# Sixteen-row triangular inverses in quads of rows, in a two-layer decoder trunk

## The chip, the cores and the metric

The kernel runs on one core of a Trainium2 chip. The metric is the device time of one execution in microseconds (us). Before the change it is 1115.59 us, the median of three runs (1115.23 to 1119.18 us).

Five engines work side by side on the core: PE (TensorE, matrix products, with its weight loads listed as PEld), DVE (VectorE), ACT (ScalarE), POOL (GpSimd) and SP (SyncE, which here only issues DMA transfers). Each engine executes its own instructions strictly in the order in which the program lists them, so an instruction that waits holds up everything listed behind it on the same engine.

## The reference

The program computes a decoder trunk of two layers over a sequence of 1024 tokens with 1024 channels. The even layer runs two mixers side by side: an RWKV-7 time mixing (8 heads of 64 channels) and a chunked spatial gate; the odd layer is a sliding-window attention. The change touches the RWKV-7 part alone, whose core is a recurrence over time:

```python
def step(S, inp):
    r_t, w_t, k_t, v_t, kk_t, a_t = inp
    sa = jnp.einsum('bhvk,bhk->bhv', S, -kk_t)
    S = (S * w_t[:, :, None, :]
         + sa[..., None] * (kk_t * a_t)[:, :, None, :]
         + v_t[..., None] * k_t[:, :, None, :])
    y_t = jnp.einsum('bhvk,bhk->bhv', S, r_t)
    return S, y_t
```

The kernel does not step through time. It cuts the sequence into chunks of 64 tokens, and inside a chunk the term with `sa` makes every token depend on the ones before it through a unit lower triangular 64 x 64 matrix. That matrix has to be inverted once per chunk and head. The inverse is built from 16 x 16 diagonal blocks, which are inverted first, and put together by matrix products. How the 16 x 16 blocks are inverted is what changes.

## The kernel before

**The stages.** The first 100 us load x, the conditioning and the first weights. From about 100 us to 630 us the even layer's input projections and the RWKV-7 and gate mixers run together. From 630 us on come the even layer's output projection (tile `op`), the odd layer's projections and attention, and the last output projection.

**The units.** The RWKV-7 work is cut into eight units: four pairs of heads times two halves of the sequence (512 tokens, eight chunks). Each unit goes through `front` (elementwise preparation of tiles `BK`, `AR`, `SV`, `BR`, `PA`), `solve` (the triangular inverse), `prep`, `scan` (the hop from chunk to chunk through PSUM tile `chain`) and `post`.

**The solve of a unit.** PE makes the 64 x 64 matrices (tiles `A` and `pM`). ACT copies the diagonal 16 x 16 blocks into `Dg`. DVE transposes them into `LN` (L638), picks `Lf` out of it (L643, L644), sets its diagonal to one (L645), and then goes through the rows 1 to 15: one `tensor_tensor` product of the row of `Lf` with the inverse's rows so far, written to the scratch tile `pr` (L650), and one `tensor_reduce` that sums it into row i of the inverse `LT` (L651). Each instruction needs the one before it. Then DVE transposes to `Tm`, masks to `ZT` (L655) and transposes to `Zq` (L658). PE multiplies (`pM<-ZT,Dg`), ACT copies to `M0`, PE multiplies again (`pM<-Zq,M`), DVE adds into `Zq` (L680) and transposes to `Tq` (L682), and PE goes on with `pM<-Tq,N`. The unit's matrices lie on the 128 partitions, 16 x 16 elements per partition for `Lf` and 16 x 8 for `LT`.

**What sets the order.** PE's instructions are listed in an order that the program plans itself while it is built. `drive()` runs nine generator threads by priority; a thread that has issued some work yields the delay after which it wants to go on, read from the table `LAT`, on a planner's clock that counts only the matrix products issued. While the solve thread is waiting, the lowest thread, `stream()`, fills in projection products (`pproj`, three per weight block, 128 x 512). The entry `qt2` is the delay between the product that the solve issues first (`p<-SV,AV`, L118) and `pM<-ZT,Dg`, that is, the time that the planner allows for the DVE's inverse. The order on DVE, ACT, POOL and SP is made by the framework's scheduler, which gives the instructions of front, solve, prep and post a higher priority than the rest.

**The other names that the prediction uses.** The gate mixer's thread makes `gvn` (normalisation, finished on DVE by `vn`, L826), `lnb` and `mix` (finished on DVE by `mx`, L841, and `uT`, L842) on PE. A thread for the conditioning loads rows of `ada` into one buffer (`araw`, L854), adds them up on DVE (`adacc`, L857) and sends the sum through PE (`adac`, `adag`; the latter is copied out by ACT as `adacc`, L868). All of `gvn`, `lnb`, `mix`, `adac` and `adag` write to one single PSUM buffer (tag "g"), so each has to wait until the one before has been read. In `front`, `kt`, `kb` and `bkt` are PE transposes of tiles that DVE makes. The output projection `op` starts as soon as the projections are through; its inputs `whi`/`wlo` are split by ACT (L245) and DVE (L246) from `wraw`, which is loaded from `y0d` in DRAM.

Of the kernel before, what the change touches and what calls it, by code (L numbers as in the profile page):

```python
# [11 lines left out]
F32 = mybir.dt.float32  # L12
# [3 lines left out]
ALU = mybir.AluOpType  # L16
AX = mybir.AxisListType
# [3 lines left out]
P = 128  # L21
# [33 lines left out]
NC2 = CONSTS["alibi"]  # L55


LAT = {"debt": 0.7, "share": 0.4, "p1": 2.31, "uw": 3.0, "mq": 4.0, "f0": 0.5, "sv0": 4.0, "wo": 2.31, "x1": 6.0, "yf": 7.85, "fetch": 3.85, "unit_norm": 12.0, "c81": 4.0, "qt1": 1.5, "bkt": 1.0, "qt2": 20.0, "qt3": 1.65, "qt4": 1.77, "qt5": 1.2, "qt6": 1.0, "yn": 12.0, "gm_tail1": 1.0, "gm_tail2": 12.0, "lnb": 1.0, "do_ada1": 4.5, "pick1": 0.5, "hop": 1.3, "ada": 8.0}


def _consts():
    c = np.zeros((P, NCON), np.float32)

    def put(name, a):
        c[:, CONSTS[name]:CONSTS[name] + a.shape[1]] = a

    r = np.arange(P)
    blk = (r[:, None] // 64) == (r[None, :] // 64)
    put("ident", np.eye(P))
    put("cblk", np.eye(P) - blk / 64.0)  # L70
    put("oblk", blk)
    s = r[:, None] % 64
    t = np.arange(64)[None, :]
    put("mr", t >= s)
    put("ma", t > s)
    rep = r % 32 // 16
    lt = np.zeros((P, 16, 8))
    for ch in range(8):
        lt[r, rep + 2 * ch, ch] = 1.0
    put("lt16", lt.reshape(P, 128))  # L80
    lane = r % 16 // 8
    put("m01", np.stack([lane == 0, lane == 1], 1))
    put("bm", np.stack([rep == 0, rep == 1], 1))
    put("tri", r[None, :] >= r[:, None])
    put("sel", np.stack([r < 64, r >= 64], 1))
    q = np.arange(128)[:, None]
    kj = np.arange(256)[None, :]
    dist = q + 128 - kj
    put("alibi", np.where((dist >= 0) & (dist < 128), dist, BIG))
    return c  # L90


@with_exitstack
def tile_kernel(ctx, tc, x, cons, par, rows, ada, ada0, ew, wup, sgw, sgb, ewo, ow, owo, out, dbg=None):
# [29 lines left out]
    V = nc.vector  # L124
# [341 lines left out]
    rsol = res.enter_context(tc.tile_pool(name="rsol", bufs=1, side="right", reuse_waits="tile"))  # L466
# [133 lines left out]
    def solve(un):  # L600
# [14 lines left out]
        for g in range(2):  # L615
            cg = slice(g * 4, g * 4 + 4)
            pts = [pm("A"), pM()]
            for i in range(4):
                c = g * 4 + i
# [3 lines left out]
            for hd in range(2):  # L623
                os = rows2[1 - hd]
                p4 = pts[hd].rearrange("p (c t) -> p c t", t=P)
# [11 lines left out]
        LN = rsol.tile([P, 16, 32], F32, name="LN", tag="LN", bufs=1)  # L637
        V.transpose(LN, Dg.rearrange("p x t -> p t x").unsqueeze(2).to_broadcast([P, 16, 2, 16]))  # L638
        LT = rsol.tile([P, 16, 8], F32, name="LT", tag="LT", bufs=1)
        S.activation(LT.rearrange("p a b -> p (a b)"), RC("lt16", 128), AF.Copy)  # L640
        m01 = RC("m01", 2)
        Lf = qt("Lf")
        V.tensor_scalar(out=Lf, in0=LN[:, :, 0:16], scalar1=m01[:, 0:1], scalar2=None, op0=ALU.mult)  # L643
        V.scalar_tensor_tensor(out=Lf, in0=LN[:, :, 16:32], scalar=m01[:, 1:2], in1=Lf, op0=ALU.mult, op1=ALU.add)  # L644
        V.memset(Lf.rearrange("p a b -> p (a b)")[:, 0:256:17], 1.0)  # L645
        LTt = LT.rearrange("p i c -> p c i")
        for i in range(1, 16):
            nc_ = i // 2 + 1
            pr = rsol.tile([P, 8, 16], F32, name="pr", tag="pr", bufs=1)
            V.tensor_tensor(out=pr[:, 0:nc_, 0:i + 1], in0=Lf[:, i:i + 1, 0:i + 1].to_broadcast([P, nc_, i + 1]), in1=LTt[:, 0:nc_, 0:i + 1], op=ALU.mult)  # L650
            V.tensor_reduce(out=LT[:, i, 0:nc_], in_=pr[:, 0:nc_, 0:i + 1], axis=AX.X, op=ALU.add)  # L651
        Tm = qt("Tm")
        V.transpose(Tm.rearrange("p x (k r) -> p k r x", r=2), LTt.unsqueeze(2).to_broadcast([P, 8, 2, 16]))
        ZT = qt("ZT", (8, 32))
# [1 line left out]
                        in1=RC("bm", 2).unsqueeze(2).unsqueeze(3).to_broadcast([P, 2, 8, 16]), op=ALU.mult)  # L656
# [10 lines left out]
        p1 = pM()  # L667
        p2 = p1[:, 256:384].rearrange("p (c t) -> p c t", t=16)
        for c in range(8):
            for qd in range(4):  # L670
                a = qd * 32
# [4 lines left out]
        for c in range(8):  # L676
            for qd in range(4):
                a = qd * 32
# [15 lines left out]
        p1 = pM()  # L694
        p1v = p1.rearrange("p (c t) -> p c t", t=64)
        for c in range(8):
            for hd in range(2):
                a, b = hd * 64, hd * 64 + 32
# [5 lines left out]
        for c in range(8):  # L704
            for hd in range(2):
                a, b = hd * 64, hd * 64 + 32
# [587 lines left out]
    wo = []  # L1294
# [116 lines left out]
```

## Time and profile before

| | |
|---|---|
| runs (us) | 1115.59, 1119.18, 1115.23 |
| the profiled execution (us) | 1115.7 |
| its span, first to last instruction (us) | 1113.9 |
| mean granted TensorE clock | 0.979 |
| PE busy | 1031.2 us, 93% of the span |
| DVE busy | 720.1 us, 65% |
| ACT busy | 526.3 us, 47% |
| POOL busy | 389.0 us, 35% |

In an answer of the profile a row of instructions reads: start in us from the beginning of the span, duration in us, engine, line of the source, operation, output tile <- input tiles, shape, how many were merged (x...), and in brackets how long the engine stood idle before it and what ended that. A row of waits reads: engine, instruction and line <- what it waited for: us in total, how often, the longest. Consecutive matrix products overlap, so a row's duration can be longer than the distance to the next row. The profiled time (1115.7 us) is its span plus 1.8 us, and lies 0.1 us above the median of the runs.

### The profile page before, as it was taken

What the parts mean: (1) busy time and instruction counts of PE and PEld (TensorE: products, weight loads), DVE (VectorE), ACT (ScalarE), POOL (GpSimd) and SP (SyncE); (2) the same over time, 40 slices, a digit from 0 to 9 for tenths busy, and PEclk for the clock granted to TensorE, in tenths of its full rate; (3) what the DMA queues carried; (4) which work ended last, traced back from release to release, by engine and by line L of the source; (5) the groups of instructions that cost most, each with busy time, mean ns of one, the idle gap of its engine ahead of it and who ended that gap; (6) DMA issues with size and microseconds to landing.
All of it is one profiled execution on the core that took longest, in us unless ns stands there. A gap on an engine that the chain in (4) does not pass through costs nothing.

```text
span 1113.9 us, 20597 instructions
## 1 busy us (share of the span) xinstructions
PE 1031.2 (93%) x7800; PEld 839.5 (75%) x7800; DVE 720.1 (65%) x1682; ACT 526.3 (47%) x1252; POOL 389.0 (35%) x490
## 2 busy tenths in 40 slices
PE   3899898899998998989999899999999999989997
PEld 2677676777776786767878688878888888878886
DVE  5865858595869585694744576764565644478754
ACT  5575434554454435544332322335565644487521
POOL 3642414240335122252423200034554544467201
PEclk8799999999999999999999899999999999999999
DMA  8710212112222121123324443321110111252121
GB/s 304 271 27 20 77 59 67 44 63 67 68 79 65 58 86 49 58 69 121 96 73 155 143 142 123 123 72 39 39 39 20 39 39 38 72 165 70 65 94 56
DMA packets 55130, 93.41 MB, mean 84 GB/s; under 512 B 5748, under 2 KB 15988, under 8 KB 55032
## 3 DMA queue, kind: packets, MB, share of 16 engines
q1 hardware_dynamic: 45032, 77.10, 21.3%
q10 hardware_dynamic: 10000, 15.01, 4.1%
q8 instruction: 61, 1.00, 0.4%
q14 instruction: 37, 0.30, 0.1%
HBM read 79.49 MB, written 12.59 MB: 83 GB/s over the span
## 4 chain that ended last, share of the span: by engine, by line
PE 71%; DVE 17%; ACT 5%; issue 3%; DMA 3%; POOL 2%; ACTq 0%; POOLq 0%; SPq 0%; DVEq 0%
PE pproj L118 35%; PE op L118 16%; DVE acc L371 2%; PE po L118 2%; PE pS L118 2%; PE pT L1222 2%; PE pM L118 2%; DVE pr L650 2%; PE py L118 1%; ACT Dg L632 1%; PE uw L118 1%; PE pn L118 1%; DVE LT L651 1%; PE chain L118 1%; PE A L118 1%
## 5 line engine op out<-in xcount | busy, mean ns | idle before, releaser
L118 PE MATMUL pproj<-hi,whi 128*128 128x512 f32 x704 | 284.5, 404 | 0.7 <-ACT vt L1176 0.7
L118 PE MATMUL pproj<-lo,whi 128*128 128x512 f32 x704 | 284.0, 403 | 0.0
L118 PE MATMUL pproj<-hi,wlo 128*128 128x512 f32 x704 | 283.4, 403 | 0.0
L246 POOL TENSOR_TENSOR wlo<-wraw,whi 128x512 fp32r<-128x512 f32 x86 | 114.7, 1353 | 181.2 <-ACT whi L245 180.3
L118 PEld LDWEIGHTS pproj<-hi,whi 128*128 128x128 f32 x704 | 133.7, 190 | 26.8 <-issue 1.7
L118 PEld LDWEIGHTS pproj<-hi,wlo 128*128 128x128 f32 x704 | 133.3, 189 | 25.2 <-issue 1.0
L118 PEld LDWEIGHTS pproj<-lo,whi 128*128 128x128 f32 x704 | 133.5, 190 | 24.4 <-issue 0.9
L245 ACT ACTIVATE whi<-wraw 128x512 fp32r<-128x512 f32 x102 | 58.7, 622 | 66.8 <-PE htp L122 31.6
L118 PE MATMUL op<-wo,whi 128*128 128x512 f32 x256 | 81.9, 401 | 0.0
L1212 ACT ACTIVATE Sx<-Sx,nm 128x257 f32<-128x257 f32 (+1 forms) x128 | 62.3, 489 | 27.2 <-DVE nm L1208 25.1
L1208 DVE CUSTOM_DVE_ANT_0 Sx<-pS,bias,nsink 128x256 f32<-128x256 f32 (+1 forms) x128 | 53.5, 463 | 30.4 <-PE pS L118 29.2
L1216 POOL TENSOR_SCALAR Sx<-Sx,rc 128x256 f32<-128x256 f32 (+1 forms) x128 | 60.8, 491 | 26.3 <-DVE rc L1214 23.7
L1228 DVE TENSOR_TENSOR PL<-pT,PH 128x512 fp32r<-128x512 f32 (+1 forms) x64 | 41.6, 655 | 30.1 <-ACT PH L1227 29.5
L118 PEld LDWEIGHTS op<-wo,whi 128*128 128x128 f32 x256 | 48.8, 191 | 11.8 <-issue 0.3
L857 DVE SCALAR_TENSOR_TENSOR adacc<-araw,cond,adacc 128x512 f32<-128x512 f32 x56 | 47.1, 840 | 11.3 <-DMA araw<-ada 11.1
L118 PE MATMUL op<-hi,yl 128*128 128x512 f32 (+1 forms) x136 | 51.7, 380 | 0.4 <-DVE yl L1327 0.4
L118 PE MATMUL op<-hi,yh 128*128 128x512 f32 (+1 forms) x136 | 51.7, 380 | 0.4 <-ACT yh L1326 0.4
L118 PE MATMUL op<-wo,wlo 128*128 128x512 f32 x128 | 51.9, 405 | 0.2 <-DVE wlo L246 0.2
L118 PE MATMUL op<-lo,yh 128*128 128x512 f32 (+1 forms) x136 | 51.6, 379 | 0.0
L213 POOL TENSOR_TENSOR st<-st,nhalf 128x1 f32<-128x1 f32 x16 | 10.4, 652 | 104.9 <-DVE st L212 104.9
L650 DVE TENSOR_TENSOR pr<-Lf,LT 128x2 f32<-128x2 f32 (+14 forms) x120 | 43.8, 365 | 2.6
L1227 ACT ACTIVATE PH<-pT 128x512 fp32r<-128x512 f32 (+1 forms) x64 | 35.7, 563 | 17.7 <-PE pT L1222 16.4
(311 smaller groups left out, 2172.1 us busy)
## 6 DMA issues: line engine op xcount, KB each, us to landing
araw<-ada SPq DMA_DIRECT2D x64, 256.0 KB, 2.7
wraw<-ew SPq DMA_DIRECT2D x50, 256.0 KB, 3.1
wraw<-ow SPq DMA_DIRECT2D x36, 256.0 KB, 2.8
adaraw<-ada SPq DMA_DIRECT2D x16, 512.0 KB, 4.8
x<-x SPq DMA_DIRECT2D x8, 512.0 KB, 6.7
woraw<-ewo SPq DMA_DIRECT2D x16, 256.0 KB, 3.0
xr<-x ACTq DMA_DIRECT2D x16, 256.0 KB, 3.1
wraw<-y0d SPq DMA_DIRECT2D x16, 256.0 KB, 3.1
```

The source lines that it names most:

```text
L118: last[0] = nc.tensor.matmul(out, lhsT=lhsT, rhs=rhs, **kw).ins
L245: a = S.activation(hi[:, gs, :], raws[g], AF.Copy)
L246: b = E.tensor_tensor(out=lo[:, gs, :], in0=raws[g], in1=hi[:, gs, :].bitcast(F32), op=ALU.subtract)
L371: V.scalar_tensor_tensor(out=acc, in0=raw[:, i], scalar=c, in1=acc, op0=ALU.mult, op1=ALU.add)
L650: V.tensor_tensor(out=pr[:, 0:nc_, 0:i + 1], in0=Lf[:, i:i + 1, 0:i + 1].to_broadcast([P, nc_, i + 1]), in1=LTt[:, 0:nc_, 0:i + 1], op=ALU ...
L857: op = V.scalar_tensor_tensor(out=acc, in0=raw, scalar=cond[:, k:k + 1], in1=acc, op0=ALU.mult, op1=ALU.add)
L1208: V.tensor_tensor_reduce(out=Sx[:, e, off:2 * P], in0=pS3[:, e, 0:nk], in1=bias[e][:, off:], scale=1.0, scalar=nsink[:, hd:hd + 1], op0=AL ...
L1212: S.activation(pr[:, e, off:2 * P + 1], Sx[:, e, off:2 * P + 1], AF.Exp, bias=nm[:, e:e + 1], scale=-1.0, accum_out=sm[:, e:e + 1])
L1216: G.tensor_scalar(out=pr[:, e, off:2 * P], in0=pr[:, e, off:2 * P], scalar1=rc[:, e:e + 1], scalar2=0.5, op0=ALU.mult, op1=ALU.mult)
L1222: nc.tensor.transpose(pT4[:, kb, e, :], pr[:, e, kb * P:(kb + 1) * P], ident)
L1227: S.activation(PH[:, ks, :], pT2[:, ks, :], AF.Copy)
L1228: V.tensor_tensor(out=PL[:, ks, :], in0=pT2[:, ks, :], in1=PH[:, ks, :].bitcast(F32), op=ALU.subtract)
```

## The change

Fifteen rows, one after the other, become four quads of rows. First the diagonal of `Lf` is set to zero, and with three more memsets what lies above it inside each 4 x 4 diagonal block. Then rows are combined so that each quad's own 4 x 4 block is resolved in `Lf` itself: one product and one add for odd rows from even rows, and for each of two columns two products and one add for the last two rows of each quad from its first two (eight instructions, over all quads at once). The diagonal is set to one. Then each quad needs one product over its four rows and all columns up to its end (4 x n x w elements, with w = 4, 8, 12, 16 and n = 2, 4, 6, 8, so 32, 128, 288 and 512) and one `tensor_reduce`. The scratch is now the tile `LN`, whose contents are used up by then. The planner's entry `qt2` goes from 20.0 to 18.

```diff
--- before.py
+++ after.py
@@ -55,7 +55,7 @@
 NC2 = CONSTS["alibi"]
 
 
-LAT = {"debt": 0.7, "share": 0.4, "p1": 2.31, "uw": 3.0, "mq": 4.0, "f0": 0.5, "sv0": 4.0, "wo": 2.31, "x1": 6.0, "yf": 7.85, "fetch": 3.85, "unit_norm": 12.0, "c81": 4.0, "qt1": 1.5, "bkt": 1.0, "qt2": 20.0, "qt3": 1.65, "qt4": 1.77, "qt5": 1.2, "qt6": 1.0, "yn": 12.0, "gm_tail1": 1.0, "gm_tail2": 12.0, "lnb": 1.0, "do_ada1": 4.5, "pick1": 0.5, "hop": 1.3, "ada": 8.0}
+LAT = {"debt": 0.7, "share": 0.4, "p1": 2.31, "uw": 3.0, "mq": 4.0, "f0": 0.5, "sv0": 4.0, "wo": 2.31, "x1": 6.0, "yf": 7.85, "fetch": 3.85, "unit_norm": 12.0, "c81": 4.0, "qt1": 1.5, "bkt": 1.0, "qt2": 18, "qt3": 1.65, "qt4": 1.77, "qt5": 1.2, "qt6": 1.0, "yn": 12.0, "gm_tail1": 1.0, "gm_tail2": 12.0, "lnb": 1.0, "do_ada1": 4.5, "pick1": 0.5, "hop": 1.3, "ada": 8.0}
 
 
 def _consts():
@@ -88,6 +88,11 @@
     dist = q + 128 - kj
     put("alibi", np.where((dist >= 0) & (dist < 128), dist, BIG))
     return c
+
+
+def bass_upper(a, r):
+
+    return bass.AP(tensor=a.tensor, offset=a.offset + 17 * r + 1, ap=[a.ap[0], [68, 4], [1, 3 - r]])
 
 
 @with_exitstack
@@ -642,13 +647,30 @@
         Lf = qt("Lf")
         V.tensor_scalar(out=Lf, in0=LN[:, :, 0:16], scalar1=m01[:, 0:1], scalar2=None, op0=ALU.mult)
         V.scalar_tensor_tensor(out=Lf, in0=LN[:, :, 16:32], scalar=m01[:, 1:2], in1=Lf, op0=ALU.mult, op1=ALU.add)
+        Lff = Lf.rearrange("p a b -> p (a b)")
+        V.memset(Lff[:, 0:256:17], 0.0)
+        for r in range(3):
+            V.memset(bass_upper(Lff, r), 0.0)
+        ev = Lf.rearrange("p (k r) c -> p k r c", r=2)
+        pr = LN.rearrange("p a b -> p (a b)")
+        t2 = pr[:, 0:128].rearrange("p (k c) -> p k c", c=16)
+        d2 = Lf.rearrange("p a b -> p (a b)")[:, 16:256:34]
+        V.tensor_tensor(out=t2, in0=ev[:, :, 0, :], in1=d2.unsqueeze(2).to_broadcast([P, 8, 16]), op=ALU.mult)
+        V.tensor_tensor(out=ev[:, :, 1, :], in0=ev[:, :, 1, :], in1=t2, op=ALU.add)
+        qd4 = Lf.rearrange("p (q r) c -> p q r c", r=4)
+        for j in range(2):
+            for r in range(2):
+                dj = Lf.rearrange("p a b -> p (a b)")[:, (2 + r) * 16 + j:256:68]
+                tj = pr[:, (2 * j + r) * 64:(2 * j + r) * 64 + 64].rearrange("p (q c) -> p q c", c=16)
+                V.tensor_tensor(out=tj, in0=qd4[:, :, j, :], in1=dj.unsqueeze(2).to_broadcast([P, 4, 16]), op=ALU.mult)
+            V.tensor_tensor(out=qd4[:, :, 2:4, :], in0=qd4[:, :, 2:4, :], in1=pr[:, j * 128:j * 128 + 128].rearrange("p (r q c) -> p q r c", r=2, c=16), op=ALU.add)
         V.memset(Lf.rearrange("p a b -> p (a b)")[:, 0:256:17], 1.0)
         LTt = LT.rearrange("p i c -> p c i")
-        for i in range(1, 16):
-            nc_ = i // 2 + 1
-            pr = rsol.tile([P, 8, 16], F32, name="pr", tag="pr", bufs=1)
-            V.tensor_tensor(out=pr[:, 0:nc_, 0:i + 1], in0=Lf[:, i:i + 1, 0:i + 1].to_broadcast([P, nc_, i + 1]), in1=LTt[:, 0:nc_, 0:i + 1], op=ALU.mult)
-            V.tensor_reduce(out=LT[:, i, 0:nc_], in_=pr[:, 0:nc_, 0:i + 1], axis=AX.X, op=ALU.add)
+        for q in range(4):
+            w, n = 4 * q + 4, 2 * q + 2
+            p4 = pr[:, 0:4 * n * w].rearrange("p (r c i) -> p r c i", r=4, c=n)
+            V.tensor_tensor(out=p4, in0=Lf[:, 4 * q:w, 0:w].unsqueeze(2).to_broadcast([P, 4, n, w]), in1=LTt[:, 0:n, 0:w].unsqueeze(1).to_broadcast([P, 4, n, w]), op=ALU.mult)
+            V.tensor_reduce(out=LT[:, 4 * q:w, 0:n], in_=p4, axis=AX.X, op=ALU.add)
         Tm = qt("Tm")
         V.transpose(Tm.rearrange("p x (k r) -> p k r x", r=2), LTt.unsqueeze(2).to_broadcast([P, 8, 2, 16]))
         ZT = qt("ZT", (8, 32))
```

The change moves the instructions on all engines of the stage from 100 us to 630 us. Three places matter below; lines after the change stand 5 to 22 further down in the source.

The end of the chain in the last unit (unit 7) on DVE. Before:

```order
L651 TENSOR_REDUCE LT<-pr 128x7
L857 SCALAR_TENSOR_TENSOR adacc<-araw,cond,adacc 128x512
L757 SCALAR_TENSOR_TENSOR Sst<-chain,dC,PA 128x64
L650 TENSOR_TENSOR pr<-Lf,LT 128x7x14
L651 TENSOR_REDUCE LT<-pr 128x7
L650 TENSOR_TENSOR pr<-Lf,LT 128x8x15
L651 TENSOR_REDUCE LT<-pr 128x8
L489 TENSOR_REDUCE nsy<-sqy 128x8
L650 TENSOR_TENSOR pr<-Lf,LT 128x128
```

and in the changed kernel:

```order
L848 TENSOR_TENSOR vn<-gvn,grs 128x512
L672 TENSOR_TENSOR LN<-Lf,LT 128x128
L673 TENSOR_REDUCE LT<-LN 128x4x4
L779 SCALAR_TENSOR_TENSOR PA<-chain,dC,PA 128x64
L672 TENSOR_TENSOR LN<-Lf,LT 128x288
L673 TENSOR_REDUCE LT<-LN 128x4x6
L672 TENSOR_TENSOR LN<-Lf,LT 128x512
L779 SCALAR_TENSOR_TENSOR PA<-chain,dC,PA 128x64
L673 TENSOR_REDUCE LT<-LN 128x32
```

Products of up to 8 x 16 elements with a reduction each have become products of up to 4 x 8 x 16; other work is listed between them in both.

PE in unit 6, shortly before `pM<-ZT,Dg`, where the conditioning and the gate mixer meet. Before:

```order
L118 MATMUL pproj<-lo,whi 128x512
L122 MATMUL bkt<-con,BK 128x128 x4
L118 MATMUL adag<-adacc,ones 1x512
L118 MATMUL mix<-sgwt,vn 64x128 x8
L118 MATMUL pproj<-hi,wlo 128x512
```

and in the changed kernel, around the same `mix`:

```order
L123 MATMUL pM<-Zq,M_5177 32x16 x32
L123 MATMUL pproj<-hi,wlo 128x512
L123 MATMUL pproj<-hi,whi 128x512
L123 MATMUL mix<-sgwt,vn 64x128 x8
L123 MATMUL pproj<-lo,whi 128x512
```

The `adag` that stood directly ahead of `mix` now comes 53 rows behind it.

PE where the projections end and the output projection begins. Before:

```order
L118 MATMUL pproj<-lo,whi 128x512
L118 MATMUL pproj<-hi,wlo 128x512
L118 MATMUL adag<-adacc,ones 1x512
L118 MATMUL mix<-sgwt,vn 64x128 x8
L118 MATMUL op<-wo,whi 128x512 x2
L118 MATMUL op<-wo,wlo 128x512
```

and in the changed kernel:

```order
L123 MATMUL pproj<-hi,wlo 128x512
L123 MATMUL op<-wo,whi 128x512 x2
L123 MATMUL op<-wo,wlo 128x512
L123 MATMUL op<-wo,whi 128x512 x2
L123 MATMUL op<-wo,wlo 128x512
L123 MATMUL op<-wo,whi 128x512
L123 MATMUL mix<-sgwt,vn 64x128 x8
L123 MATMUL op<-wo,whi 128x512
L123 MATMUL op<-wo,wlo 128x512
L123 MATMUL op<-wo,whi 128x512 x2
L123 MATMUL op<-wo,wlo 128x512
L123 MATMUL adag<-adacc,ones 1x512
```

The last `mix` and the last `adag` have moved from in front of the output projection to behind its first products.

## The prediction

> **What bounds the kernel now.** I first read busy time by stretches, since a share over the whole span mixes stages.
>
> ```profile
> 100.00:630.00 530.00, 486.05 (x5021) 382.58 (x5017) 357.47 (x811) 238.57 (x539) 167.25 (x133) 0.99 0.24 77
> 630.00:980.00 350.00, 349.22 (x1798) 294.51 (x1799) 204.69 (x544) 164.41 (x428) 125.16 (x226) 1.00 0.21 68
> ```
>
> The columns are stretch, its length, then busy time of PE, PEld, DVE, ACT and POOL. From 630 us on PE has no gap worth having, and the change adds nothing there. From 100 to 630 us, where the inverses run, PE is busy for 486.05 of 530 us. Its own work does not change, so the change can only move the other 44 us, and DVE, at 67%, matters as far as PE waits for it. Next I read PE's waits:
>
> ```profile
> PE pn L118 <- DVE AR L735: 7.2, 8, 2.7
> PE kt L122 <- ACT th L509: 5.8, 7, 1.1
> PE kb L122 <- DVE sqk L493: 4.4, 2, 2.7
> PE adag L118 <- DVE vn L826: 3.6, 1, 3.6
> PE mix L118 <- ACT adacc L868: 3.2, 2, 2.3
> PE mix L118 <- DVE bst L833: 2.7, 1, 2.7
> PE bkt L122 <- DVE BK L544: 2.7, 1, 2.7
> PE pM L118 <- DVE Tq L682: 2.5, 3, 1.2
> PE gvn L118 <- ACT adacc L868: 1.0, 1, 1.0
> PE kb L122 <- DVE LT L651: 1.0, 1, 1.0
> ```
>
> No row has PE waiting for `ZT`, the end of the chain that is rebuilt: the planner lists enough projections ahead of it. The waits are of two other kinds. Some are for DVE work that stands in line with the chain (`sqk`, `BK`, `bst`, and the row with `LT`). Others come from where the planner put things: `adag`, `mix` and `gvn` share one PSUM buffer and are sometimes listed too close.
>
> **The chain on DVE.**
>
> ```profile
> L650 DVE TENSOR_TENSOR pr<-Lf,LT 128x2 f32<-128x2 f32 (+14 forms) x120 | 43.8, 365 | 2.6
> L651 DVE TENSOR_REDUCE LT<-pr 128x1 f32<-128x2 f32 (+14 forms) x120 | 24.4, 203 | 2.7
> 538.01 0.07 DVE L645 MEMSET Lf<- 128x16 f32 x1
> 538.11 0.16 DVE L650 TENSOR_TENSOR pr<-Lf,LT 128x2 f32<-128x2 f32 x1
> 538.31 0.16 DVE L651 TENSOR_REDUCE LT<-pr 128x1 f32<-128x2 f32 x1
> 538.50 0.17 DVE L650 TENSOR_TENSOR pr<-Lf,LT 128x6 f32<-128x6 f32 x1
> 546.60 0.33 DVE L650 TENSOR_TENSOR pr<-Lf,LT 128x98 f32<-128x98 f32 x1
> 547.25 1.11 DVE L650 TENSOR_TENSOR pr<-Lf,LT 128x120 f32<-128x120 f32 x1
> 550.87 0.28 DVE L651 TENSOR_REDUCE LT<-pr 128x8 f32<-128x128 f32 x1
> 551.91 0.43 DVE L655 TENSOR_TENSOR ZT<-Tm,rcon 128x256 f32<-128x256 f32 x1
> 565.45 0.28 DVE L680 TENSOR_TENSOR Zq<-Zq,pM 128x128 f32<-128x128 f32 x1
> ```
>
> Before, a unit costs (43.8 + 24.4) / 8 = 8.5 us of DVE time. The rows give the law behind it. A product takes 0.17 us at 6 elements and 0.33 at 98, so 0.16 us plus 1.74 ns an element; a reduction (0.16 at 2, 0.28 at 128) 0.16 plus 0.95 ns. The fifteen products of a unit hold 779 elements: 15 x 0.16 + 779 x 0.00174 = 3.75 us, and the reductions 2.4 + 0.74 = 3.1 us. Eight units of products should be 30.0 us and are 43.8: the missing 13.8 us are collisions, such as the 1.11 us row, 0.12 us per product or 1.7 us per unit.
>
> After, a unit has four such products with 32 + 128 + 288 + 512 = 960 elements (0.64 + 1.67 = 2.31 us), four reductions (0.64 + 0.91 = 1.55), one product and three adds of 128 elements (0.28 each by the `Zq` row, 1.12), four products of 64, for which I take 0.25 (1.0), and four more memsets (0.28): 6.26 us against 6.85. The padded quads multiply more elements than the rows did, so this is only 0.6 us. Collisions go with the number of products and adds, 12 instead of 15: 1.4 us for 1.7, another 0.3. From the end of one instruction of the chain to the start of the next that needs it pass 0.04 us (538.27 to 538.31), with about ten fewer of them 0.4 us. Together **1.3 us a unit**, 10 us of DVE time in eight. Bounds: if the new products don't pay 1.74 ns an element but the 1.0 that the `ZT` row leaves (0.43 us for 256, less 0.16), 0.7 us more, and without any collision 1.4 more: 3.4. If small products cost the law of the strided ones and collisions grow with product time, about 0.3.
>
> [...]
>
> **Does PE now reach `ZT` too early?** `qt2` falls by 2.0, so the planner lists `pM<-ZT,Dg` about 2 us sooner after the solve's first product. Where the slack is least:
>
> ```profile
> 133.90 0.42 DVE L655 TENSOR_TENSOR ZT<-Tm,rcon 128x256 f32<-128x256 f32 x1
> 135.35 0.75 PE L118 MATMUL pM<-ZT,Dg 16*32 16x32 f32 x64
> 366.70 0.43 DVE L655 TENSOR_TENSOR ZT<-Tm,rcon 128x256 f32<-128x256 f32 x1
> 369.13 0.75 PE L118 MATMUL pM<-ZT,Dg 16*32 16x32 f32 x64
> 499.71 0.42 DVE L655 TENSOR_TENSOR ZT<-Tm,rcon 128x256 f32<-128x256 f32 x1
> 502.70 0.50 PE L118 MATMUL pM<-ZT,Dg 16*32 16x32 f32 x35
> ```
>
> Units 0, 4 and 6 have 1.0, 2.0 and 2.6 us from the end of `ZT` to the product; the other five have 5.5 us or more. Less 2.0, plus 1.3, that is 0.3, 1.3 and 1.9: no wait, so **0**, at the edge in unit 0.
>
> After `ZT` the chain goes on through ACT and DVE to `Tq`, for which PE already waits 2.5 us in three units. The new order leaves fewer projections between `pM<-Zq,M` and `pM<-Tq,N`: 3 with two small groups instead of 10 in unit 0, 5 instead of 7 in unit 1, 9 instead of 10 in unit 3, 9 without the three products of `front` in unit 5, 5 with `mix` instead of 11 in unit 6. A projection row is 9.75 / 42 = 0.23 us (first row below). That is some 0.5 + 0.5 + 0.2 + 0.6 + 0.4 = **+2.2 us**.
>
> **What the new order takes away.** The hand-over to the output projection:
>
> ```profile
> 603.14 9.75 PE pproj L118 x42
> 617.68 1.05 PE L118 MATMUL gvn<-con,vT 128*128 128x128 f32 x8
> 624.02 0.69 DVE L826 TENSOR_TENSOR vn<-gvn,grs 128x512 f32<-128x512 f32 x1 [0.81 <-POOL grs L824]
> 624.85 1.02 PE L118 MATMUL adag<-adacc,ones 128*1 128x512 f32 x2 [3.62 <-DVE vn L826]
> 626.78 1.98 PE L118 MATMUL mix<-sgwt,vn 128*64 128x128 f32 x16 [0.91 <-ACT adacc L868]
> 630.09 0.79 PE L118 MATMUL op<-wo,wlo 128*128 128x512 f32 x1 [0.18 <-DVE wlo L246]
> ```
>
> `gvn` fills the shared buffer at 617.68 and `vn` empties it at 624.71, 7.0 us later. `adag` stands in front of the output projection and waits; PE loses 3.62 + 0.91 + 0.18 = 4.7 us. In the new order thirteen projections and eight rows of `op` stand between `gvn` and the next user: 0.9 + 21 x 0.23 = 5.8 us, so about 1.2 us stay, and `adag` comes later still. This holds if `op` can start: it needs only the first half of its first block by then, whose fetch SP lists well ahead. The second half is fetched behind two loads for `adacc`, which reuse one buffer. `uT` ends 3.3 us after the last-but-one `mix` starts (614.54 to 617.79), so this fetch leaves at about 4.0, lands 3.1 later at 7.1, is split by ACT and, after `vn`, by DVE at about 9.6; PE needs it at 10.0.
>
> ```profile
> araw<-ada SPq DMA_DIRECT2D x64, 256.0 KB, 2.7
> wraw<-y0d SPq DMA_DIRECT2D x16, 256.0 KB, 3.1
> 614.54 1.09 PE L118 MATMUL mix<-sgwt,vn 128*64 128x128 f32 x16
> 616.81 0.98 DVE L842 TENSOR_TENSOR uT<-mx,uT 128x512 f32<-128x512 f32 x1
> ```
>
> So **-3.5 us**. The other waits on the shared buffer (2.3 of the row `mix` <- `adacc`, 1.0 of `gvn` <- `adacc`) come from an `adag` directly ahead; in the new order 42 rows or more stand between `adag` and the user before it, and at least six between `adag` and the user after it, about 2.6 us, where `adag` with ACT's copy takes 1.9 here (624.85 to 626.78): **-3.3 us**.
>
> The waits behind the chain on DVE fall by what the chain ahead of them saves: `bkt` (2.7) stands behind all of it in unit 0, -1.3; the two `kb` <- `sqk`, `mix` <- `bst` and `kb` <- `LT` in its midst, half of it each, -2.6. **-3.9 us.** The rows `pn` <- `AR` and `kt` <- `th` recur in every unit and stay. A redrawn order also makes new neighbours that I can't see; an unlucky one in the present order costs 1 to 3 us, and I allow **+1.0**.
>
> **Sum.** From the profiled execution's 1115.7 us (span 1113.9, 0.1 above the median of the runs): +2.2 - 3.5 - 3.3 - 3.9 + 1.0 = -7.5, so **1108.2 us**. Of it 6.8 come from the new order and 3.9 from a shorter chain. With a saving of 0.3 us a unit, 2.7 us of unlucky neighbours and half of the hand-over it is 1114.5; with 2.4 us (7.0 off the waits behind the chain), no new neighbours and no price at `Tq`, 1102: the likeliest case's own range.
>
> **The rivals.** *Waits only change places.* The order is redrawn in all eight units, and what is gained at the shared buffer comes back as other waits; only the chain's part is left: 1115.7 - 3.9 + 2.2 + 1.0 = 1115 us. For it: the waits are spread over ten kinds, none over 7.2 us. Against: the hand-over is at a fixed place, and its rows are seen to move.
>
> *The chain does not get shorter, but PE comes sooner.* The quads multiply 23% more elements, in products of up to 1.05 us; if these collide with POOL twice more a unit (the 1.11 us row is 0.75 above its law), the chain is 1.5 us longer. Units 0, 4 and 6 then wait for `ZT` by 2.0 + 1.5 less their slack: 2.5, 1.5, 0.9. The waits behind the chain grow by as much as I let them shrink, +4.5. With 2.2 and 1.0 and the order's -6.8 that makes +5.8: 1121.5 us, and slower than before from about 0.5 us of lengthening on. For it: 13.8 us at about 0.75 each are 18 collisions in 120 products now. Against: there are fewer of them. [...]
>
> *The chain is 3.4 us shorter*, the upper bound above. Then `bkt` and one `kb` no longer wait, the other waits behind the chain fall to 1 us or nothing (8.7 us in all), and nothing is lost at `Tq`: 1115.7 - 6.8 - 8.7 = 1100 us. Against it stands the 98-element row.
>
> **How the numbers follow.** Forecast 0.53, places 0.22, slower 0.13, much shorter 0.12. Less than 0.5% (5.6 us) can't be told from no change. Faster than 1110.0 are two thirds of the forecast (0.35), all of the last and a little of the second: 0.5. Slower than 1121.2 is a bit over half of the third and 0.03 for what I overlook: 0.11; the rest, 0.39, is the same. The range of 8 in 10 leaves out the worse half of the slower case and the better half of the fast one: 1101 to 1120 us.
>
> **What would show it.** In the changed profile: the 512-element product near 1.05 us (0.7 if strides cost nothing); DVE about 10 us less busy from 100 to 630 us; no row of PE waiting for `ZT`; PE idle at the hand-over about 1 us; `mix` <- `adacc` gone; `pM` <- `Tq` at 4 to 5 us. I am wrong if `ZT` is waited for, if the hand-over keeps 3 us or more, or if a wait that is not in the list above exceeds 3 us.

## The result and the profile after

The changed kernel takes 1122.71 us (median of 20 runs, 1116.09 to 1128.45) against 1115.30 us before (median of 20, 1111.70 to 1120.26): a ratio of 1.0062, 95% interval 1.0048 to 1.0075. It is slower; 1108.2 us, faster, was predicted. The profiled execution took 1126.2 us, so it is one of the longer ones.

The stretches of the kernel before (two rows) and of the changed kernel (two rows), in the columns of the prediction: stretch, length, busy time of PE, PEld, DVE, ACT and POOL, mean granted clock of PE, DMA share, GB/s.

```profile
100.00:700.00 600.00, 555.96 (x5336) 439.39 (x5333) 404.41 (x913) 257.42 (x581) 170.02 (x138) 0.99 0.26 83
100.00:1113.90 1013.90, 958.64 (x7483) 781.86 (x7479) 652.73 (x1570) 469.16 (x1138) 341.27 (x443) 0.99 0.23 75
```

```profile
100.00:700.00 600.00, 556.11 (x5269) 437.53 (x5269) 391.24 (x815) 254.37 (x574) 174.53 (x137) 0.96 0.26 80
100.00:1124.40 1024.40, 970.04 (x7469) 789.46 (x7468) 647.91 (x1490) 469.22 (x1138) 344.91 (x443) 0.97 0.23 74
```

The span grew by 10.5 us, but PE does not stand idle longer: 1013.90 - 958.64 = 55.3 us before, 1024.40 - 970.04 = 54.4 after. It is *busy* for 11.4 us more, with the same products. The clock column says why: 0.99 against 0.96 over 600 us. In windows of 1 us the granted clock is either 1.00, or 0.50 for a while. Three such stretches of the changed kernel, with the PE rows they begin at (in brackets how long PE waited, and for what):

```profile
246.49 0.76 PE L123 MATMUL bon<-qh,oblr 128*128 128x512 f32 x2 [1.87 <-ACT yc L805]
305.70 1.06 PE L123 MATMUL pM<-Tq,N 32*32 32x32 f32 x32 [3.00 <-DVE Tq L704]
643.37 1.87 PE L123 MATMUL adag<-adacc,ones 128*1 128x512 f32 x2 [2.45 <-DVE mx L863]
```

```profile
247.00:248.00 1.00, 1.00 (x3) 0.33 (x2) 0.96 (x2) 0.98 (x3) 0.00 (x0) 0.52 0.01 2
248.00:249.00 1.00, 1.00 (x33) 0.93 (x32) 0.70 (x2) 0.01 (x1) 0.00 (x0) 0.50 0.12 47
...
304.00:305.00 1.00, 0.00 (x0) 0.00 (x0) 0.99 (x2) 0.00 (x0) 0.64 (x1) 1.00 0.85 201
305.00:306.00 1.00, 0.30 (x12) 0.33 (x14) 0.99 (x3) 0.00 (x0) 0.00 (x0) 0.53 0.86 285
...
325.00:326.00 1.00, 1.00 (x4) 0.79 (x4) 0.00 (x0) 0.00 (x0) 0.00 (x0) 0.72 0.00 0
326.00:327.00 1.00, 1.00 (x8) 0.56 (x9) 0.00 (x0) 0.00 (x0) 0.00 (x0) 1.00 0.00 0
```

Behind the wait for `Tq` the clock stays halved from 305 to 326 us although PE is busy for 17.10 of the 19 us from 306 to 325. Twice (1 - clock), summed over the 1-us windows from 100 to 700 us, gives the time at half rate: 17.0 us before (in four places), 47.8 us after: 10.2 behind `bon` at 247, 20.5 behind `Tq` at 305, 6.8 at 369 (`gvn`), 6.8 at 499 (`mix`) and 3.4 at 643 (`adag`). In all the kernels below PE's busy time from 100 us on follows this sum; a straight line through the eleven without added products gives 950.2 us plus 0.41 us for each microsecond at half rate (within 1.5 us for nine of them, 2.3 for the other two). By that line the 30.8 us more at half rate are about 12.6 us, where PE was busy for 11.4 us more: the half rate accounts for the difference between these two executions.

They are not a typical pair. Each run lists the mean granted clock of its whole execution: 0.9774 in the mean over 61 runs of the kernel before, 0.9730 over the 20 of the changed one, which is 50 and 60 us at half rate (twice 1 - clock, times the span). So the typical difference is about 10 us, not 30.8, and by the line about 4 us of the 7.4 between the medians. The profiled execution of the change had only 3.4 us of its half rate in the first 100 us, where all the other profiles have 24 to 27, and so the more behind them.

PE's waits in the changed kernel, the rows that bear on the list that the prediction began with (in us: total, times, longest):

```profile
PE pM L123 <- DVE Tq L704: 6.2, 4, 3.0
PE gvn L123 <- ACT vT L926: 5.0, 2, 4.5
PE pn L123 <- DVE AR L757: 5.0, 8, 0.7
PE mix L123 <- DVE bst L855: 3.0, 1, 3.0
PE adag L123 <- DVE mx L863: 2.4, 1, 2.4
PE kb L127 <- DVE sqk L498: 2.0, 3, 1.2
PE bon L123 <- ACT yc L805: 1.9, 1, 1.9
PE uw L123 <- POOL qh L555: 1.6, 1, 1.6
PE op L123 <- ACT whi L250: 1.2, 1, 1.2
```

No row names `ZT`; `mix` <- `adacc` and `bkt` <- `BK` are gone. In their place stand `gvn` <- `vT`, `bon` <- `yc`, `uw` <- `qh`, and a dearer `Tq`.

Three of the new chain's groups on DVE (busy us, mean ns of one | idle before):

```profile
L665 DVE TENSOR_TENSOR LN<-Lf 128x64 f32<-128x64 f32 x32 | 11.1, 387 | 0.2
L672 DVE TENSOR_TENSOR LN<-Lf,LT 128x512 f32<-128x512 f32 x8 | 9.1, 1136 | 0.1
L666 DVE TENSOR_TENSOR Lf<-Lf,LN 128x128 f32<-128x128 f32 x16 | 7.3, 453 | 0.2
```

The largest product takes 1.14 us (1.08 at the least), where 1.05 was predicted. All groups of the quads together are about 60 us, 7.5 us a unit against 8.5 before.

### The profile page after: what moved, and what is told of

The parts are those of the page before. It is cut to its first block, busy times and chain, and to the rows that moved or that the text cites. A ratio compares the mean times of both kernels' runs of the same rounds, so it can differ in the third digit from the quotient of the medians.

```text
span 1124.4 us, 20521 instructions
## 1 busy us (share of the span) xinstructions
PE 1044.3 (93%) x7800; PEld 848.0 (75%) x7800; DVE 715.2 (64%) x1602; ACT 527.1 (47%) x1252; POOL 392.8 (35%) x490
## 4 chain that ended last, share of the span: by engine, by line
PE 74%; DVE 16%; ACT 5%; issue 2%; DMA 2%; POOL 1%; ACTq 0%; POOLq 0%; DVEq 0%; SPq 0%
PE pproj L123 37%; PE op L123 16%; PE pS L123 3%; PE po L123 2%; DVE acc L376 2%; PE pT L1244 2%; PE pM L123 2%; PE uw L123 2%; PE py L123 1%; DVE LN L672 1%; ACT Dg L637 1%; PE adac L123 1%; PE pn L123 1%; DVE LN L665 1%; PE A L123 1%
## 5 line engine op out<-in xcount | busy, mean ns | idle before, releaser
L879 DVE SCALAR_TENSOR_TENSOR adacc<-araw,cond,adacc 128x512 f32<-128x512 f32 x56 | 50.0, 893 | 19.9 <-DMA araw<-ada 19.8
L1249 ACT ACTIVATE PH<-pT 128x512 fp32r<-128x512 f32 (+1 forms) x64 | 35.7, 563 | 17.1 <-PE pT L1244 16.0
L1264 POOL TENSOR_TENSOR y<-y,cm 128x256 f32<-128x256 f32 x32 | 24.1, 752 | 51.7 <-DVE cm L1262 51.6
```

The lines of the kernel that those rows point to most:

```text
L879: op = V.scalar_tensor_tensor(out=acc, in0=raw, scalar=cond[:, k:k + 1], in1=acc, op0=ALU.mult, op1=ALU.add)
L1249: S.activation(PH[:, ks, :], pT2[:, ks, :], AF.Copy)
L1264: G.tensor_tensor(out=yv, in0=yv, in1=cm.rearrange("p b q -> p (b q)"), op=ALU.mult)
```

## The experiments

Times are medians, ratios are to the kernel before, run on the same chip. "Idle" is PE's idle time from 100 us to the end of the span, "half rate" the sum described above, both from the one profiled execution. Beside the experiments the kernel before took 1116.3 to 1116.6 us. The two kernels with added products stand further down.

| kernel | us | ratio (95%) | idle | half rate |
|---|---|---|---|---|
| before | 1115.3 | 1 | 55.3 | 17.0 |
| the change (quads, delay 18) | 1122.7 | 1.0062 (1.0048 to 1.0075) | 54.4 | 47.8 |
| quads, delay 20 | 1110.5 | 0.9954 (0.9939 to 0.9969) | 52.1 | 17.1 |
| rows, delay 18 | 1132.6 | 1.0166 (1.0137 to 1.0195) | 63.4 | 37.5 |
| no rows, delay 20 | 1099.2 | 0.9858 (0.9837 to 0.9879) | 43.7 | 13.6 |
| quads, delay 19 | 1128.8 | 1.0101 (1.0076 to 1.0127) | 62.4 | 34.1 |
| quads, delay 21 | 1118.0 | 1.0017 (1.0001 to 1.0033) | 56.7 | 13.7 |
| the change, `adag` in its own buffer | 1115.5 | 0.9999 (0.9978 to 1.0019) | 52.2 | 17.1 |
| quads, delay 20, `adag` in its own buffer | 1108.2 | 0.9923 (0.9906 to 0.9940) | 50.8 | 10.2 |
| rows, delay 20, `adag` in its own buffer | 1111.9 | 0.9963 (0.9943 to 0.9982) | 51.4 | 27.2 |
| the change, profiled again | 1122.3 | 1.0047 (1.0025 to 1.0069) | 55.6 | 40.9 |

The change does two things: it rebuilds the chain on DVE, and by `qt2` 20 -> 18 it makes the planner redraw the order of all engines. The first theory was that the redrawn order loses the time, through new waits and the half rate behind them; the rival, that the quads themselves do. The first two runs make one half of the change each.

**The quads in the order of before.**

```diff
-"bkt": 1.0, "qt2": 18, "qt3": 1.65
+"bkt": 1.0, "qt2": 20.0, "qt3": 1.65
```

> The quads with the planner's entry qt2 back at 20.0, which lists PE's instructions row for row as before the change. Theory 1 (the loss is in PE's redrawn order: waits of 3 to 4.5 us that PE did not have there, and the half clock granted behind them): no slower than before, 1112 to 1115.5 us, with DVE some 5 to 10 us less busy from 100 to 630 us. Theory 2 (the quads themselves are slower on DVE, by collisions with POOL, and hold up what PE waits for): 1120 us or more. The prediction's own terms for the shorter chain (3.9 us off the waits behind it): 1111 to 1112 us.

Measured: 1110.52 us, 0.9954 (0.9939 to 0.9969), some 5 us faster than before. PE's list is row for row that of before. The quads do not cost time, they save it; the rival falls.

**The rows in the order of the change.**

```diff
-"bkt": 1.0, "qt2": 20.0, "qt3": 1.65
+"bkt": 1.0, "qt2": 18, "qt3": 1.65
```

(to the kernel before)

> The fifteen rows as before, with qt2 at 18, which lists PE's instructions row for row as in the changed kernel. Theory 1: as slow as the change or slower, 1122 to 1128 us, because the order brings the waits. Theory 2: no slower than before, 1113 to 1117 us.

Measured: 1132.63 us, 1.0166 (1.0137 to 1.0195). The order alone costs 16 to 18 us with the rows, 12.2 us with the quads (1122.71 - 1110.52). With the rows PE does reach `ZT` too early:

```profile
381.50 1.06 PE L118 MATMUL pM<-ZT,Dg 16*32 16x32 f32 x64 [2.19 <-DVE ZT L655]
517.11 0.75 PE L118 MATMUL pM<-ZT,Dg 16*32 16x32 f32 x64 [3.99 <-DVE ZT L655]
PE pM L118 <- DVE ZT L655: 6.8, 3, 4.0
```

These 6.8 us the quads take away: their chain is short enough for the delay of 18, the rows' is not.

**No chain at all.** This kernel leaves out the fifteen rows, so the 16 x 16 inverses are not computed; the rest is that of before.

```diff
-        for i in range(1, 16):
...
-            V.tensor_reduce(out=LT[:, i, 0:nc_], in_=pr[:, 0:nc_, 0:i + 1], axis=AX.X, op=ALU.add)
```

> The kernel before with its order, but the fifteen rows left out altogether: LT keeps its starting value, so the inverse is not computed. It bounds from above what any shortening of the chain can bring under this order: 68 us less DVE time. Theory 1 and 2 alike: the waits behind the chain (10.8 us before) nearly go and no half clock follows the one before kb: 1100 to 1107 us. If the chain hardly matters to PE: 1112 us or more.

Measured: 1099.19 us, 0.9858. A chain of no length is worth some 16 to 17 us in the order of before. The quads, which cut DVE's busy time in the chain from 8.5 to 7.5 us a unit, got 5 of them.

**The change with PE kept busy in its waits.** Products with a matrix of zeros, added to groups that are open anyway, stand ahead of the waits at 246, 306, 371 and 498 us and at the hand-over.

```diff
+    def fill(pt, rhs, i, at):
+        nfill[i] += 1
+        for _ in range(at.get(nfill[i], 0)):
+            nc.tensor.matmul(pt, lhsT=zr, rhs=rhs, start=False, stop=False)
```

> The changed kernel with products of a zero matrix added into the accumulation that is open (they add nothing) directly ahead of six waits of PE: 6, 11, 17 and 11 ahead of bon, Tq, gvn and mix, 4 and 9 ahead of the second half of the first output block and of adag, sized to end within the wait. The waits stay as long as they were; only PE is not idle in them. Theory 1 with the half clock as its main cost: the stretches at clock 0.50 behind these waits vanish, 1108 to 1114 us. If the waits alone cost the time and the clock nothing: 1122 us, or slightly more.

Measured: 1118.97 us, 1.0030 (1.0006 to 1.0054), 3.7 us less than the change although PE has more to do. The half rate fell from 47.8 to 17.1 us in the profiled executions, and by the clocks of all runs (0.9860, the mean of 12) from 60 to 31 us; by the line above that is 12 us, of which most was given back. PE came to `gvn` at 361.65 and not at 371.08, but then stood before DVE's line at the next places:

```profile
PE gvn L123 <- DVE mx L876: 5.0, 2, 4.0
PE bkt L127 <- DVE BK L562: 1.9, 1, 1.9
```

This kernel does not isolate the half rate, though: besides the added products, the framework's scheduler drew up DVE's list anew. Near 500 us `mx`, for which PE then waits 4.0 us, now stands behind three more instructions of the chain (a reduction, the largest product and its reduction). How much of what was given back is that and how much work of DVE that the half rate hid before is not shown.

**One step more and one step back.** Is 18 too early, or is every redrawn order another draw?

```diff
-"bkt": 1.0, "qt2": 18, "qt3": 1.65
+"bkt": 1.0, "qt2": 19, "qt3": 1.65
```

> The quads with the listed delay at 19, between the kernel before (20) and the change (18). If the loss grows with how early the order puts the product behind the solve ("too early"), the time lies between the two measured ones, 1110.5 and 1122.7 us, near 1116, and PE waits for Tq or ZT longer than at 20 (more than 2 us in all) and less than at 18 (6.2 us). If instead every redrawn order brings its own waits at places that have nothing to do with the solve ("a new draw"), the time is not tied to 19 being in the middle: it may lie anywhere from 1108 to 1126 us, and the PE waits over 1.9 us name other tiles than in either. In both theories the half-rate stretches of the clock follow the waits: about 10 us of them for each 5 us of time lost.

Measured: 1128.84 us, 1.0101 (1.0076 to 1.0127), outside the two times that it lies between, with 62.4 us idle. New places wait: `bkt` <- `BK` 4.20 us at 365, `mq` and `pn` near 446 and 450 us, and for once with the quads `ZT`, 2.0 us at 511, which at 18 is not waited for.

```diff
-"bkt": 1.0, "qt2": 18, "qt3": 1.65
+"bkt": 1.0, "qt2": 21, "qt3": 1.65
```

> The quads with the listed delay at 21, one more than before's. "Too early": later is no worse for the waits, so 1108 to 1111 us, with no PE wait for Tq over 1.5 us. "A new draw": the order is redrawn here too, though nothing is asked for earlier, so the time is again anywhere from 1108 to 1126 us, with 20 to 48 us of half-rate clock before the stage's end as the waits of this order fall.

Measured: 1118.03 us, 1.0017 (1.0001 to 1.0033), 7.5 us slower than with 20 though `pM<-ZT,Dg` is asked for later. Its largest wait behind the first 100 us is for `Tq` all the same:

```profile
201.82 1.07 PE L123 MATMUL pM<-Tq,N 32*32 32x32 f32 x32 [4.60 <-DVE Tq L704]
```

"Too early" does not explain it: at 18, 19, 20 and 21 the quads take 1122.7, 1128.8, 1110.5 and 1118.0 us. The order of before is the best of the four, and a half-rate sum of 13.7 us with 56.7 us idle (in a profiled execution of 1115.0 us, the shortest of the twelve) shows that a draw can be bad in waits alone.

**The hand-over.** In the change the second half of the first fetched block comes late, DVE gets behind with it, and `adag` waits for the buffer that the last `mix` holds until `mx` has read it (PE row 643.37 above). From the changed kernel, SP, ACT and DVE there:

```profile
633.62 1.50 SPq L1085 DMA_DIRECT2D wraw<-y0d x3
639.51 0.63 ACT L250 ACTIVATE whi<-wraw 128x512 fp32r<-128x512 f32 x1 [3.85 <-DMA wraw<-y0d]
640.17 0.69 DVE L251 TENSOR_TENSOR wlo<-wraw,whi 128x512 fp32r<-128x512 f32 x1 [3.23 <-ACT whi L250]
641.77 0.69 DVE L1078 TENSOR_TENSOR gate<-gate,gateb 128x512 f32<-128x512 f32 x1 [0.90 <-DMA gateb<-rows]
642.57 0.75 DVE L863 SCALAR_TENSOR_TENSOR mx<-mix,prm,bst 128x512 f32<-128x512 f32 x1
```

The next kernels put the last `adag` into the PSUM buffer of `chain`, which has long ended there (its last product is at 605.71 us). The list of PE is unchanged; on DVE the scheduler moved `gate` behind `mx` and `uT`, so that `mx` too comes a little sooner, and the two effects are not told apart.

```diff
-                pt = pg("adag")
+                pt = psc("adag") if (layer, n) == (1, 1) else pg("adag")
```

In the change:

> The change, with the last adag in the PSUM buffer of the long finished chain and not in the one that the last mix holds until mx is done. If the hand-over of the new order is what I read it to be, adag's wait for mx (2.45 us) and the half clock behind it (3.4 us at half rate, 1.7 us lost) go: 1118.5 us against the change's 1122.7, and from the first op to the end 485 us and not 489.6. If only the wait moves (to op behind adag, for the late half of the fetched block), 1121 to 1123 us and 488 to 490 us. If the fetched block's late landing is the whole of it, the op wait of 1.2 us stays and adag's is replaced by one of about the same length for whi or wlo.

Measured: 1115.50 us, 0.9999 (0.9978 to 1.0019): 7 us less than the change (difference of the ratios 0.0063, about 0.0024 either way). From the first `op` to the end it takes 1109.50 - 623.91 = 485.6 us, the change 1124.40 - 634.80 = 489.6: 4.0 us, as expected. `adag` waits no more, and what is left is the late block:

```profile
629.35 0.73 PE L123 MATMUL op<-wo,whi 128*128 128x512 f32 x2 [1.14 <-ACT whi L250]
630.01 1.02 PE L123 MATMUL adag<-adacc,ones 128*1 128x512 f32 x2
```

Ahead of the hand-over the two kernels list the same on every engine. There the two profiled executions differ by 10.9 us, which goes with the half rate (below); of the 7 us between the medians 3 are left for it.

In the order of before, with the quads:

> The quads in the order of before (delay 20), with the last adag in that other buffer. Its wait of 3.60 us for vn is then no wait of adag: adag runs at once, and mix, which needs vn itself, takes the wait, but no longer behind adag (1.02 us) and its copy (0.92 us of wait). So the hand-over is 1.9 to 2.5 us shorter: 1108.2 us against 1110.5 for the quads in this order. If the wait is whole again at mix, with the half clock behind it as before (20 us of it in all), not more than this; if adag's early start lets the clock stay at full rate, another 1 to 2 us, 1106.5.

Measured: 1108.23 us, 0.9923 (0.9906 to 0.9940), ahead of both before and the change, and the fastest but for the one without the rows. `adag` runs at 617.00 without a wait, and `mix` takes it over, shorter and 2.7 us earlier than with the quads alone (623.40):

```profile
620.69 1.26 PE L123 MATMUL mix<-sgwt,vn 128*64 128x128 f32 x16 [2.66 <-DVE vn L848]
622.05 1.22 PE L123 MATMUL op<-wo,whi 128*128 128x512 f32 x2
```

With the rows, the buffer alone changed:

> The kernel before with nothing altered but the buffer of the last adag. If its hand-over (adag's wait for vn, adag, its copy, then mix) is a queue on one buffer, whatever the rows do, this is 2 to 2.5 us faster than before, as with the quads (1110.5 to 1108.2): ratio 0.998. If the gain with the quads came from their shorter chain, there is none here: ratio 1.000.

Measured: 1111.87 us, 0.9963 (0.9943 to 0.9982), about 4 us. The queue on the one buffer is a cost of before too, and does not need the quads. The gains of 4 us here and of 2 to 3 with the quads lie within each other's interval.

**The same program again.**

> The change once more, unaltered, for a second profile of it. If the length of the half-rate stretch behind a wait is fixed by the wait, the same waits (1.9 us at bon, 3.0 at Tq, 4.5 at gvn, 3.0 at mix, 2.4 at adag) have the same stretches behind them as in the first profile (10.2, 20.5, 6.8, 6.8 and 3.4 us) and the profiled execution takes 1124 to 1127 us. If the same wait can be followed by a stretch of 0, 3.4 or more us from one execution to the next, as the profile of the change with adag in its own buffer suggests (none, 3.4, 6.8 and 3.4 us behind the first four), the sum is another here, and the time follows it at about half a microsecond for each microsecond of half rate.

Measured: 1122.32 us median, the profiled execution 1124.0. The five waits named are the same to 0.4 us, the half rate is not: 40.9 us in all, and behind the wait for `Tq` 6.8 us where it was 20.5. From this profile:

```profile
305.93 0.72 PE L123 MATMUL pM<-Tq,N 32*32 32x32 f32 x32 [2.99 <-DVE Tq L704]
305.00:306.00 1.00, 0.07 (x5) 0.10 (x7) 0.97 (x4) 0.00 (x0) 0.00 (x0) 1.00 0.80 297
306.00:307.00 1.00, 1.00 (x34) 0.94 (x36) 0.42 (x1) 0.31 (x1) 0.00 (x0) 0.73 0.62 182
314.00:315.00 1.00, 1.00 (x8) 0.90 (x7) 0.26 (x1) 0.68 (x2) 0.00 (x0) 1.00 0.00 0
```

In the first profile the clock fell at 305 us, here at 306, against the same wait. In the change with `adag` in its own buffer the same wait (2.98 us) was followed by 3.4 us, and the one at `bon` (1.88 us) by none. So one and the same wait was followed by stretches of different length, and at `bon` once by none.

These three executions are also the cleanest measure of its price, since they list the same up to the hand-over and wait the same. In each PE starts `bon` between 246.49 and 246.94 us; the next long wait behind `Tq` ends at `gvn`, in the first profile of the change, the second, and the one with `adag` in its own buffer:

```profile
371.08 2.08 PE L123 MATMUL gvn<-con,vT 128*128 128x128 f32 x8 [4.49 <-ACT vT L926]
365.88 2.08 PE L123 MATMUL gvn<-con,vT 128*128 128x128 f32 x8 [4.51 <-ACT vT L926]
360.32 2.08 PE L123 MATMUL gvn<-con,vT 128*128 128x128 f32 x8 [4.51 <-ACT vT L926]
```

From `bon` to `gvn` they take 124.6, 119.3 and 113.4 us. PE stands idle for 11.7 us in each; at half rate it is for 31.9, 18.5 and 5.4 us. Here 0.42 us of time go with each microsecond at half rate, and nothing is given back. The draws may also be why the times of the change spread over 12 us and those of the quads in the order of before over 2.7 (1109.35 to 1112.03, eight runs).

**Filling the best kernel.** Eight zero products ahead of `gvn` near 350 us and twelve ahead of `mix` near 480 us, in the quads at delay 20 with `adag` in its own buffer.

> The quads in the order of before with adag in its own buffer (1108.2 us), and products with a matrix of zeros added at two places so that PE does not stand idle there: 8 ahead of gvn and kb near 350 us (waits of 1.40 and 2.52 us, 3.4 us of half clock behind them), 12 ahead of mix near 480 us (wait 3.33 us, 3.4 us of half clock behind it). If the half clock is a cost of its own, it goes there and the kernel takes 1.7 to 3.4 us less: 1105 to 1106.5 us. If the next wait takes it back, as with most of what the fillers brought in the change, 1108 to 1109.

Measured: 1110.62 us, 0.9943 (0.9929 to 0.9958), no faster than without; the 2.4 us between the medians are not clear of noise (difference of the ratios 0.0020, about 0.0023 either way). The half rate from 100 to 700 us is 10.2 us in both: the stretch near 355 is gone, but the one at the first `op` products is longer. The wait at `mix` fell from 3.33 to 0.60 us and came back behind it at `gvn`, with the half rate:

```profile
485.91 1.27 PE L123 MATMUL gvn<-con,vT 128*128 128x128 f32 x8 [3.67 <-DVE mx L876]
```

`mix` came no later (479.79 us, and 479.97 without the added products), but DVE's list was drawn up anew here too: `mx`, for which `gvn` waits, now stands behind four more of the chain's instructions and starts at 485.11 instead of 482.58. So this kernel does not show what filling alone is worth.

## Why the prediction was wrong

The step that failed is the share of the new order. The sum gave it -3.6 us (+2.2 - 3.5 - 3.3 + 1.0); with the quads in both orders the runs show +12.2 us (1110.52 to 1122.71). Its waits came out larger than their terms, and the half rate behind them had no term at all. The chain's share of -3.9 us came out as -5.

**The chain: right, and its gain too.** The product law (1.05 us predicted, 1.14 measured for 512 elements) held; the quads' DVE time is 1.0 us a unit shorter, where 0.9 was worked out (0.6 and 0.3 from fewer collisions). The term of -3.9 us is the run of the quads in the order of before: PE's idle time falls from 55.3 to 52.1, the median by about 5; the rest goes with the half rate (50 to 41 us by the clocks of all runs), which the term did not have. Of the five waits that the term names, 10.8 us became 7.3, though not one by one: `bkt` and one `kb` went to nothing, the other three grew by 0.4 to 0.9 us. The rival "the chain does not get shorter, but PE comes sooner" has 1121.5 us, next to the 1122.7 measured, but by luck: the chain did get shorter and nothing waits for `ZT`. The rival "3.4 us shorter" fails with its 1100 us, though from the first memset to the end of `ZT` a unit did become 3.7 us shorter in the same order (19.7 to 16.0, the mean of eight; 14.33 to 10.96 in the last). Of these only 1.1 are the chain's own rows (8.6 to 7.5 us); most of the rest is other work that no longer stands among them. No more than the 5 us came through to the time.

**No wait for `ZT`: right**, and the rows at delay 18 show the edge, 6.8 us of it.

**`Tq`, +2.2: too small.** It went from 2.5 to 6.2 us. Counting the projections in the list left out what DVE had put ahead of `Tq` in one unit. From the changed kernel:

```profile
301.65 0.28 DVE L702 TENSOR_TENSOR Zq<-Zq,pM 128x128 f32<-128x128 f32 x1
301.85 1.68 DVE L998 SCALAR_TENSOR_TENSOR gz<-bv,der,gz 128x512 f32<-128x512 f32 x1
303.56 1.54 DVE L712 COPY Z<-Zq 32x256 f32<-32x256 f32 x2
305.11 0.45 DVE L704 STREAM_TRANSPOSE Tq<-Zq 128x256 f32<-128x256 f32 x1
```

**The hand-over, -3.5: wrong.** `mix` runs without a wait, as said, but `op` then waits 1.22 us and `adag` 2.45: 3.7 of the 4.7 us are back. What failed here is the way of the second half: counted from the last-but-one `mix` (627.95), as the prediction does, it left after 5.7 us and not 4.0 (at 633.62, with two more fetches), and ACT could read it after 11.6 and not 7.1 (at 639.51, 5.9 us later and not 3.1; why it took so long is not shown). And "`adag` comes later still" took no account of what holds its buffer: `mx`, behind `wlo` and `gate` on DVE. Only seven `op` products stand between the last `mix` and this `adag`; the "42 rows or more" of the next term do not hold for it. (Ahead of `mix` the list has seven rows of `op` too, where the prediction counted eight, 0.23 us.)

**The other waits on the shared buffer, -3.3: about right in place, smaller in size.** `mix` <- `adacc` and `gvn` <- `adacc` are gone; 0.9 us of `gvn` <- `mx` came. Not all of it is the order's: in the old one the quads alone bring `mix` <- `adacc` from 3.2 to 1.6 us.

**New neighbours, +1.0: the term that was far too small.** `gvn` <- `vT` rose from 1.7 to 5.0 us, and `bon` <- `yc` (1.9) and `uw` <- `qh` (1.6) are new. The largest is a queue of three engines. ACT first, then DVE and POOL, from the changed kernel:

```profile
368.25 0.60 ACT L492 ACTIVATE sqk<-kt 128x512 f32<-128x512 f32 x1 [6.71 <-DVE BK L545]
370.43 0.60 ACT L926 ACTIVATE vT<-pproj 128x512 f32<-128x512 f32 x1 [1.58 <-DVE nsk L494]
363.15 2.55 DVE L665 TENSOR_TENSOR LN<-Lf 128x64 f32<-128x64 f32 x2
362.63 2.99 POOL L251 TENSOR_TENSOR wlo<-wraw,whi 128x512 fp32r<-128x512 f32 x2
```

`vT` takes its data from PE, where the last projection ahead of it ended at 366.15 us. It stands behind `sqk` on ACT, which waits for `BK`, which stands on DVE behind two small products of the chain that take 2.55 us together instead of 0.43 while POOL runs `wlo`. For the last 1.58 us the profile names DVE's `nsk`, which reads `sqk`; what ties `vT` to it is not shown. In sum the new order changed PE's idle time by +2.3 us against the quads in the old one (54.4 and 52.1), where -3.6 were forecast.

**What no term held: the clock.** The sum took a wait to cost its own length. The row of `mix` that the prediction quotes at the hand-over, 1.98 us for sixteen products that elsewhere take 1.09, was already one at half rate (the granted clock was 0.50 to 0.58 from 626 to 633 us of the kernel before), and it was read over. The change waits as long as before in all, but in other portions: five waits of 1.9 to 4.5 us at places with half-rate stretches behind them, 47.8 us against 17.0 in the profiled executions. In the mean of all runs the clock is 0.9730 for the change and 0.9814 for the quads in the old order (eight runs), 60 and 41 us at half rate: by 0.41 that is some 8 of the 12 us that the order costs, and 2.3 more are idle time in the profiles. Against the kernel before it is about 4 us, so that by this estimate the change would be some 3 us slower without it and not 7. The rival "waits only change places" had the idle time right and the same price missing.

What stays open: these shares are means over whole executions, the first 100 us included, and no kernel removes the half rate alone. Open too is why a stretch lasts 3.4 us in one execution and 20.5 in another behind the same wait, and how much of the 7 us between the change and the quads at delay 20, both with `adag` in its own buffer (1115.5 and 1108.2), is half rate and how much waits; the two profiles differ by only 1.4 us of idle time and 6.9 us at half rate, but that profile of the first is its shortest execution, 1111.3 us, and its times reach up to 1123.7.

## What to carry to other kernels

Before forecasting what a redrawn order does, weigh each PE wait of about 2 us and more twice, for itself and for the half rate that may follow (here up to 20.5 us behind waits of 1.9 to 4.5 us in one execution, and none behind the shortest of them in another), and read the clock column in windows of 1 us wherever a product takes about twice its usual time, as `mix` did with 1.98 us for 1.09. A change that touches both a computation and a planner's number should be timed in both halves: here the computation gave -5 us and the number took +12. And where a tile waits for a buffer and not for data, another buffer is the cheap move: some 2 to 4 us here, with the rows and with the quads. And an added instruction on one engine can move the lists of the others, so compare these before calling a run a test of one thing; the single profile of each kernel should be set against the clocks of all its runs.

## What the runs showed of the hardware

The stretches at half rate were 3.4, 6.8, 10.2 and 20.5 us long in the first profile of the change, where they began near waits of 1.9 to 4.5 us; by the straight line through the profiles each microsecond of them cost about 0.41 us of PE time. In the three executions that wait the same, the same wait was followed by 0 to 10.2 us (`bon`) and 3.4 to 20.5 us (`Tq`). Work on PE did not end a stretch at once: from 248 to 257 us of the changed kernel PE was busy for all of the 9.00 us at a clock of 0.50, from 306 to 325 us for 17.10 of 19.00.

Small DVE products took long only beside POOL's work. Of the change's 32 products of 64 elements the twenty with no POOL instruction beside them took 0.20 to 0.23 us; five took 1.20 to 1.33 us, as in the row at 363.15, and POOL was at work for at least nine tenths of each of these. Seven more with POOL beside them stayed at 0.22 to 0.26 us. No reduction of the chain took longer beside POOL (0.68 us for 512 elements with and without). The collisions did not go away with fewer instructions: against the median of the same form with no POOL work beside it, those that ran beside POOL took 13.6 us longer among the 120 products before, and 10.2 us longer among the change's 96 products and adds.
